# Layer 0's mixer: three pairs of column blocks with two seven-product units each

## The chip, the cores and the metric

The kernel runs on one core of a Trainium2 chip. The metric is the device time of one execution in microseconds (us), the median of several runs. The engines are named as in the profile: PE (TensorE's matmuls; PEld its weight loads), DVE (VectorE), ACT (ScalarE), POOL (GpSimd), SP (SyncE, which issues the weight loads).

## The reference, cut to what matters

A two-layer encoder over 256 tokens of width 2048, in fp32. Layer 0 mixes tokens by a chunked spatial gating and by attention to 256 memory tokens; layer 1 by grouped-query attention. Each layer ends with a SwiGLU FFN.

```python
h = rms_norm(x, g_mix[l])                       # (256, 2048)
z = h @ w_in_a                                  # layer 0: u 1536, v 1536, q_mem 512 columns
tok_in, q_mem = split(z, [3072])
u, v = split(gelu(tok_in), 2)
v = rms_norm(v, g_v_a)
s = einsum('gts,bcsgd->bctgd', w_spatial, v) + b_spatial
tok_out = u * s                                 # 1536 wide
mem_out = memory_attention(q_mem, mem, ...)     # 512 wide, 4 heads
x = x + concat([tok_out, mem_out]) @ w_out[l]   # 2048 x 2048
x = x + (silu(gate) * up) @ w_down[l]           # gate, up = split(rms_norm(x) @ w_gate_up[l])
```

## The kernel before, in words

**The matmul.** Activations and weights are fp32, split into two halves that TensorE takes at full speed: hi is a rounded copy, lo the rest. matmul3 (L185 to L189) makes three matmuls of a product: hi x hi, lo x hi, hi x lo. A weight tile `raw` (128 x 2048: four 128x512 pieces) is loaded by SP, its `whi` is a cast on ScalarE (L271), its `wlo` a subtraction on VectorE (L272). There are 3 buffers each of whi and wlo (W_TILES) and 4 of raw (RAW_TILES), so a half's making waits for PE to be done with the one three before it.

**Linear** (run at L288 and after) computes one block of 512 columns for both halves of the tokens (t = 0, 1) in two PSUM banks named `acc` out of four. It takes four units of four pieces of depth: 24 matmuls each, 96 a block. A tick of the program's clock passes after each 12; `later(n, f)` records work n ticks on.

**Pair** (L346 to L460) computes two neighbouring blocks, as the FFN does already. A unit is a 2 x 2 arrangement of weight pieces against a 2 x 2 arrangement of activations (two pieces of depth, two token halves). `eight` takes eight products, 24 matmuls; `seven`, for units in `fast`, takes seven, 21 matmuls, and needs sums: of weights in `prepare` (L380 to L382: T from raw, raw from T, T from raw, after which T's three pieces are halved as well as raw's four), and of activations (activation_sums, L318 to L333, from whole features that feature_sums, L825, adds up from their halves first). Products that both token halves share gather in two double banks from the pool `m`; after the last seven `inner` (L430 to L437) joins them into the tile `e`, and at the pair's end `outer` (L453 to L458) adds the four acc banks to e, which empties those banks for what comes next.

**Layer 0's mixer** runs thirteen Linears: v's three blocks, q_mem, the memory's keys and values, u's three blocks, w_out's four. v's blocks go through gelu and squares as they come (`gated`, L767 to L771); gate_rms and gate (L687 to L700) scale v and multiply it by the spatial matrices. Each of u's blocks goes through gelu on ScalarE (L787), is multiplied by the gate on VectorE (L788), and is turned (turn_u, L702): `turned` (L195) copies its 16-bit planes apart on VectorE (L200), turns them by a DMA transpose from ScalarE's queue (L201), and some ticks later copies them back (L206); `split` (L177 to L183) then makes hi (ScalarE, L181) and lo (VectorE, L182), which w_out's matmuls read. Because turning u's last block takes time, w_out's units start with the memory heads (pieces 12 to 15). The memory attention's steps are set at ticks (4, 16, 20, 28) after q_mem. add_residual (L645) adds a block of w_out to x and turns it for the FFN. The mixer's pool has 36 tiles (MIX_TILES), its `m` banks are four single ones.

**What sets the order.** The program is recorded as written, with the ticks; a scheduler then lists the instructions of each engine, by a simulated timeline of its own. On the chip each engine takes its list in that order, so an instruction that waits holds back all behind it. After layer 0's mixer comes the FFN (pairs throughout), then layer 1, not touched.

Of the kernel before, what the change touches and what calls it, by code (L numbers as in the profile page):

```python
# [10 lines left out]
F32 = mybir.dt.float32  # L11
# [6 lines left out]
P = 128  # L18
# [14 lines left out]
KC4 = 4  # L33
MIX_TILES = 36
FFN_TILES = 26
# [6 lines left out]
class Parts:  # L42


    def __init__(self):
        self.ap, self.whole = {}, {}

# [8 lines left out]
def encoder(ctx: ExitStack, tc: tile.TileContext, x, x_t, mem, mem_t, columns, w_in_a, g_v_a, spatial_t, w_in_b,  # L56
# [23 lines left out]

    def open_rooms(scope, name, tiles, banks):

        room["p"] = scope.enter_context(tc.tile_pool(name=name, bufs=tiles, reuse_waits="tile"))
        room["m"] = scope.enter_context(tc.tile_pool(name=f"ps_{name}", bufs=4 // banks, space=PS))
        room["banks"] = banks

    def banks2():
# [149 lines left out]
    def gained_pair(src, i, g, parts, keep):  # L237

        hi = keep(F32R, [P, 2, S])
        lo = keep(F32R, [P, 2, S])  # L240
        for c in range(2):
            gc = g[:, 2 * i + c:2 * i + c + 1]
            nc.scalar.activation(hi[:, c], src[:, c], AF.Copy, scale=gc)
            nc.vector.scalar_tensor_tensor(lo[:, c], src[:, c], gc, hi[:, c].bitcast(F32), ALU.mult, ALU.subtract)
            for t in range(NT):
                ts = slice(t * P, (t + 1) * P)
                parts.put(2 * i + c, t, hi[:, c, ts], lo[:, c, ts])

    class Norm:
# [68 lines left out]
    def activation_sums(a0, a1, apart=False):  # L318

        if apart:  # L320
            q = room["p"].tile([P, KC3, NB], F32, tag="T", name=nm("T"), bufs=2)[:, 0].rearrange("p (c n) -> p c n", n=P)
        else:
            q = big(F32, [P, 4, P])
# [17 lines left out]
    class Pair:  # L341
# [29 lines left out]
        def prepare(self, i):  # L371

            if i in self.ready:
                return
            raw = self.fetch(i)
            self.ready[i] = (raw,)
            if i in self.fast:
                T = room["p"].tile([P, KC3, NB], F32, tag="T", name=nm("T"), bufs=2)
                w01 = raw[:, 0].unsqueeze(1).to_broadcast([P, 2, NB])
                nc.vector.tensor_tensor(T[:, :2], raw[:, 1:4:2], w01, ALU.add)  # L380
                nc.vector.tensor_tensor(raw[:, 0], T[:, 0], raw[:, 3], ALU.add)
                nc.vector.tensor_tensor(T[:, 2], raw[:, 0], raw[:, 2], ALU.add)  # L382
                self.ready[i] = raw, T

# [278 lines left out]


    hT = Parts()
    norm = Norm()
    for l in range(DEPTH):
        scope = ExitStack()
        open_rooms(scope, f"mix{l}", MIX_TILES, 1)
        cat = Parts()  # L670
        m = Memory(l)
        if l == 0:
            w = w_in_a[0]
# [28 lines left out]
            def turn_u(us, t, c):  # L702
                def parts(whole):
                    hi, lo = split(whole, [P, 4, P])
                    for i in range(4):
# [61 lines left out]
            def gated(c, acc):  # L767
                for t in range(NT):
                    v[t][c] = big()
                    nc.scalar.activation(v[t][c], acc[t], AF.Gelu, scale=norm.r[t])  # L770
# [11 lines left out]
            m.values()  # L782
            for c in range(3):
                acc = linear(hT, w, c * NB)
# [27 lines left out]
        norm = Norm()  # L812
        units = kd if l else [(12, KC4), (0, KC4), (4, KC4), (8, KC4)]
        for j in range(4):
            acc = linear(cat, w_out[l], j * NB, units)
            add_residual(acc, j, norm, gslice("ffn", l), hF, j < 3, nc.scalar.copy if l else nc.vector.tensor_copy)
        room.clear()
        scope.close()
# [5 lines left out]

        def feature_sums(i):  # L825
            j, c = i // 2, 2 * (i % 2)
            whole = []
            for t in range(NT):
                hi, lo = hF.whole[j, t]
                a = big(F32, [P, 2, P])  # L830
                nc.vector.tensor_tensor(a, hi[:, c:c + 2].bitcast(F32), lo[:, c:c + 2].bitcast(F32), ALU.add)
                whole.append(a)
            sums[i] = activation_sums(*whole)

        for i in fast:
            later(2 + 2 * i, lambda i=i: feature_sums(i))

        hT = Parts()
        next_norm = Norm()
        for chunk in (range(0, 4), range(4, 8), range(8, 11)):  # L840
# [44 lines left out]
            for jj, g in enumerate(pairs):  # L885
                g.run(None if jj else pairs[1])
                for j in (2 * jj, 2 * jj + 1):
                    if last and l < DEPTH - 1:
                        residual_turns(j, next_norm, gslice("mix", l + 1), hT)
                    elif last:  # L890
                        for t in range(NT):
                            parts = 2 if j == 3 and t == NT - 1 else 1
                            for i in range(parts):
# [3 lines left out]
                                              X[t][j][:, cs])  # L897
        norm = next_norm
        room.clear()
        scope.close()  # L900
# [48 lines left out]
```

## Time and profile before

| what | value |
|---|---|
| median of 3 runs | 1989.67 us (1989.49 to 1989.98) |
| the profiled execution, its own time | 1992.44 us |
| its span, first to last instruction | 1990.7 us |
| granted TensorE clock | 1.0 |
| first matmul of v's second block | 28.61 us |
| of q_mem, the keys, the values | 73.60, 100.68, 122.53 us |
| of u's first, second block | 144.29, 170.59 us |
| of w_out's first, third block | 217.03, 260.55 us |
| of the FFN | 304.07 us |

In rows of the timeline the columns are start, duration, engine, line, operation, output<-inputs, and in brackets the idle time before it with what ended it. Groups give count, busy time, mean in ns, and the idle time before them. In windows come the length, the busy time (and count) of PE, PEld, DVE, ACT and POOL, the granted clock, the DMA share and GB/s. An instruction that follows another closely on DVE or ACT starts a little before that one's end as shown.

### The profile page before, as it was taken

Reading aid. Unit: us, or ns where it says so; the run is one execution under the profiler, and the core shown is the slowest. Engines: PE = TensorE matmul, PEld = TensorE weight load, DVE = VectorE, ACT = ScalarE, POOL = GpSimd, SP = SyncE. Lnnn points to the kernel's source line nnn. Section 1 sums busy time; section 2 is a strip of 40 time slices with the busy share of each in tenths; the row PEclk is TensorE's granted clock in tenths of the full one; section 3 lists DMA queues with packets and bytes.
Section 4 is the critical chain, followed back from the end, with each engine's and each line's share of the span. In section 5 each row is a group of like instructions: output and inputs, shape, how many; then the busy total and the mean of one; then the engine's idle time right before and its main releaser. Section 6 shows DMA issues by size and latency. Waiting matters only on the chain.

```text
span 1990.7 us, 24068 instructions
## 1 busy us (share of the span) xinstructions
PE 1978.8 (99%) x8913; PEld 1638.5 (82%) x8913; DVE 1648.7 (83%) x1783; ACT 1214.6 (61%) x1461; POOL 81.5 (4%) x122
## 2 busy tenths in 40 slices
PE   9999999999999999999999999999999999999998
PEld 7888888888887888888888888888888878888887
DVE  6668678998988989898676876699889889898887
ACT  8756555775546655466765755766664567644673
POOL 2300001000000000000011000010000000000000
PEclk9999999999999999999999999999999999999999
DMA  9867765676775767757866444747767667686674
GB/s 349 300 190 228 217 212 190 196 224 214 235 230 180 233 208 240 236 183 237 240 204 208 157 143 155 221 169 224 229 200 248 199 201 233 201 252 213 196 226 139
DMA packets 283495, 425.93 MB, mean 214 GB/s; under 512 B 89681, under 2 KB 89937, under 8 KB 283377
## 3 DMA queue, kind: packets, MB, share of 16 engines
q1 hardware_dynamic: 199808, 387.62, 58.6%
q10 hardware_dynamic: 78576, 19.86, 5.7%
q0 software_dynamic: 4992, 16.91, 3.8%
q8 instruction: 70, 1.15, 0.2%
q14 instruction: 49, 0.39, 0.1%
HBM read 394.45 MB, written 2.10 MB: 199 GB/s over the span
## 4 chain that ended last, share of the span: by engine, by line
PE 91%; DMA 3%; DVE 3%; issue 1%; ACT 1%; SPq 0%; DVEq 0%; ACTq 0%
PE acc L189 26%; PE acc L187 26%; PE acc L188 26%; PE m L189 4%; PE m L187 4%; PE m L188 4%; DMA a<-a 2%; DVE wlo L272 2%; DMA raw<-in_w_in_a 1%; ACT whi L271 1%; PE m L193 0%; PE m L561 0%; DMA raw<-in_w_down 0%; DMA raw<-in_w_gate_up 0%; PE m L698 0%
## 5 line engine op out<-in xcount | busy, mean ns | idle before, releaser
L272 DVE TENSOR_TENSOR wlo<-raw,whi 128x2048 fp32r<-128x2048 f32 (+2 forms) x466 | 841.7, 1823 | 214.0 <-ACT whi L271 206.9
L271 ACT CAST whi<-raw 128x2048 fp32r<-128x2048 f32 (+2 forms) x466 | 706.0, 1535 | 448.8 <-PE acc L188 317.8
L187 PE MATMUL acc<-whi,h 128*128 128x512 f32 x1440 | 561.0, 390 | 1.5 <-ACT whi L271 1.5
L188 PE MATMUL acc<-whi,h 128*128 128x512 f32 x1440 | 560.7, 389 | 0.0
L189 PE MATMUL acc<-wlo,h 128*128 128x512 f32 x1440 | 514.9, 390 | 1.3 <-DVE wlo L272 1.1
L187 PE MATMUL acc<-whi,a 128*128 128x512 f32 x999 | 388.6, 390 | 1.2 <-DVE x L458 1.2
L188 PE MATMUL acc<-whi,a 128*128 128x512 f32 x999 | 388.9, 390 | 0.0
L189 PE MATMUL acc<-wlo,a 128*128 128x512 f32 x999 | 365.5, 390 | 0.0
L189 PEld LDWEIGHTS acc<-wlo,h 128*128 128x128 f32 x1440 | 270.3, 188 | 58.8 <-DVE wlo L272 3.2
L187 PEld LDWEIGHTS acc<-whi,h 128*128 128x128 f32 x1440 | 270.4, 188 | 57.4 <-ACT whi L271 2.1
L188 PEld LDWEIGHTS acc<-whi,h 128*128 128x128 f32 x1440 | 270.4, 188 | 55.7
L187 PEld LDWEIGHTS acc<-whi,a 128*128 128x128 f32 x999 | 187.5, 188 | 40.5 <-issue 1.6
L189 PEld LDWEIGHTS acc<-wlo,a 128*128 128x128 f32 x999 | 187.6, 188 | 39.7 <-DVE wlo L272 0.9
L188 PEld LDWEIGHTS acc<-whi,a 128*128 128x128 f32 x999 | 187.6, 188 | 38.5
L271 ACT CAST whi<-T 128x1536 fp32r<-128x1536 f32 x93 | 137.8, 1482 | 120.4 <-PE acc L188 94.1
L272 DVE TENSOR_TENSOR wlo<-T,whi 128x1536 fp32r<-128x1536 f32 x93 | 163.3, 1756 | 4.7 <-PE acc L189 4.7
L380 DVE TENSOR_TENSOR T<-raw 128x1024 f32<-128x1024 f32 x93 | 113.7, 1222 | 17.2 <-DMA raw<-in_w_gate_up 17.1
L189 PE MATMUL m<-wlo,a 128*128 128x512 f32 x284 | 110.7, 390 | 0.3 <-DVE wlo L272 0.2
L187 PE MATMUL m<-whi,a 128*128 128x512 f32 x284 | 110.9, 391 | 0.1
L188 PE MATMUL m<-whi,a 128*128 128x512 f32 x284 | 110.5, 389 | 0.0
L458 DVE TENSOR_TENSOR e<-acc,e 128x512 f32<-128x512 f32 x120 | 79.5, 690 | 1.7 <-PE acc L189 1.3
L206 ACT COPY sg<-a 128x1024 uint16<-128x1024 uint16 x44 | 51.5, 1171 | 33.4 <-DMA a<-a 33.4
(145 smaller groups left out, 1520.1 us busy)
## 6 DMA issues: line engine op xcount, KB each, us to landing
raw<-in_w_gate_up SPq DMA_DIRECT2D x352, 512.0 KB, 4.4
raw<-in_w_down SPq DMA_DIRECT2D x176, 512.0 KB, 4.9
raw<-in_w_out SPq DMA_DIRECT2D x32, 1024.0 KB, 5.3
raw<-in_w_in_a SPq DMA_DIRECT2D x24, 1024.0 KB, 7.7
raw<-in_w_in_b SPq DMA_DIRECT2D x24, 1024.0 KB, 5.1
raw<-in_w_mem_kv SPq DMA_DIRECT2D x16, 1024.0 KB, 5.2
x<-e POOLq DMA_DIRECT2D x16, 512.0 KB, 5.1
a<-in_mem_t POOLq DMA_DIRECT2D x16, 256.0 KB, 4.3
```

Of the source, the lines that this page charges most:

```text
L187: nc.tensor.matmul(out, lhsT=a[0], rhs=b[0], start=start, stop=False)
L188: nc.tensor.matmul(out, lhsT=a[1], rhs=b[0], start=False, stop=False)
L189: nc.tensor.matmul(out, lhsT=a[0], rhs=b[1], start=False, stop=stop)
L206: copy(halves, back.rearrange("p (h n) -> p n h", h=2))
L271: nc.scalar.copy(hi[:, cut], raw[:, cut])
L272: nc.vector.tensor_tensor(lo[:, cut], raw[:, cut], hi[:, cut].bitcast(F32), ALU.subtract)
L380: nc.vector.tensor_tensor(T[:, :2], raw[:, 1:4:2], w01, ALU.add)
L458: nc.vector.tensor_tensor(o[t][n], self.bank[name], o[t][n], op)
```

## The change

v's second and third blocks, u's second and third, and w_out's first and second are each computed as one Pair of eight units, of which units 0 and 1 are sevens, at the fourth and sixth place (w_out: third and fourth, units 6 and 7, the memory heads, first). The sums for v and u are made from h in v's first block's wake and kept (`hsums`); those for w_out's sevens are made from u's first block (`csums`). Pairs need double banks, so the `m` pool is opened as two double banks, changed to four single ones for q_mem to u's first block, and back. v's first block is copied out of PSUM by VectorE as soon as it is done and gated later. Both of u's last blocks now come at the pair's end, and go through gelu, gate and turning together. w_out's first two blocks are added to x together. The memory attention's last step is set at tick 24 instead of 28, and u's second block is turned one tick earlier after its end. T's scratch has one buffer in the mixer. The number of PE's rows goes from 8744 to 8726, DVE's from 1550 to 1632, ACT's from 1092 to 1102; POOL has 126 and SP 389 in both. After layer 0's mixer the order is the same on all engines.

```diff
-MIX_TILES = 36
+MIX_TILES = (29, 36)
...
+    def block_sums(parts, i, apart=False):
+        whole = []
+        for t in range(NT):
+            if i in parts.pair:
+                both = [a[:, :, t * P:(t + 1) * P] for a in parts.pair[i]]
+            else:
+                both = [a[:, 2 * (i % 2):2 * (i % 2) + 2] for a in parts.whole[i // 2, t]]
+            a = big(F32, [P, 2, P])
+            nc.vector.tensor_tensor(a, both[0].bitcast(F32), both[1].bitcast(F32), ALU.add)
+            whole.append(a)
+        return activation_sums(*whole, apart)
...
+    def two(parts, sums, w, n0, order, fast):
+
+        g = Pair(parts, sums, w, n0, n0 + NB, order, fast)
+        g.run()
+        return [[g.out[t][n] for t in range(NT)] for n in range(2)]
...
-            later(7, lambda: gated(0, acc))
-            for c in (1, 2):
-                gated(c, linear(hT, w, TOK + c * NB))
+            whole = [big() for _ in range(NT)]
+            for t in range(NT):
+                nc.vector.tensor_copy(whole[t], acc[t])
+            later(7, lambda: gated(0, whole))
+            for i in range(2):
+                sums_later(hT, hsums, i, 4 + 2 * i, not i)
+            for c, acc_c in zip((1, 2), two(hT, hsums, w, TOK + NB, (2, 3, 4, 0, 5, 1, 6, 7), (0, 1))):
+                gated(c, acc_c)
+            open_banks("mix0", 1)
...
-            m.attend(linear(hT, w, 2 * TOK), norm.r, cat, (4, 16, 20, 28), True)
+            m.attend(linear(hT, w, 2 * TOK), norm.r, cat, (4, 16, 20, 24), True)
...
+                if c == 1:
+                    later(4, lambda: open_banks("mix0", 2))
+                    for i in range(2):
+                        sums_later(cat, csums, i, 10 + 2 * i)
+                    blocks = two(hT, hsums, w, NB, (2, 3, 4, 0, 5, 1, 6, 7), (0, 1))
+                acc = blocks[c - 1] if blocks else linear(hT, w, c * NB)
...
-                    later(1 + t, lambda u=u, t=t, c=c: turn_u(u, t, c))
+                    later(t + (c != 1), lambda u=u, t=t, c=c: turn_u(u, t, c))
...
+        if l == 0:
+            blocks = two(cat, csums, w_out[l], 0, (6, 7, 0, 1, 2, 3, 4, 5), (0, 1))
         for j in range(4):
-            acc = linear(cat, w_out[l], j * NB, units)
+            acc = blocks[j] if j < 2 and not l else linear(cat, w_out[l], j * NB, units)
```

Lines move by some ten: in the changed kernel whi and wlo are L283 and L284, the T sums L392 to L394, e's joining L446 to L449, its last additions L470, the two copies of turning L211 and L217 with the transpose at L212, split L192 and L193, the gelu of u L836 and its product L837, the residual L670.

**VectorE where w_out begins, before.** The names: wlo is the low half of a weight tile, `a` any 128x512 tile of the mixer (here u's last block); the first number is the tile's.

```order
L272 TENSOR_TENSOR wlo_336_1960<-raw_334_1957,whi_335_1959 128x1024 x2
L788 TENSOR_TENSOR a_321_1907<-a_321_1907,a_109_713 128x512
L200 COPY a_330_1937<-a_321_1907 128x1024
L272 TENSOR_TENSOR wlo_341_1997<-raw_339_1994,whi_340_1996 128x1024 x2
L788 TENSOR_TENSOR a_322_1910<-a_322_1910,a_110_717 128x512
L206 COPY a_321_1907<-a_331_1938 128x1024
L200 COPY a_332_1953<-a_322_1910 128x1024
L272 TENSOR_TENSOR wlo_346_2034<-raw_344_2031,whi_345_2033 128x1024 x2
L182 TENSOR_TENSOR a_338_1991<-a_321_1907,a_337_1990 128x512
L206 COPY a_322_1910<-a_333_1954 128x1024
L182 TENSOR_TENSOR a_343_2016<-a_322_1910,a_342_2015 128x512
```

**The same place after the change, rows 205 to 216** (T is the sum tile of w_out's first seven, wlo_389 its low half):

```order
L837 TENSOR_TENSOR a_354_1977<-a_354_1977,a_129_754 128x512
L837 TENSOR_TENSOR a_355_1980<-a_355_1980,a_130_758 128x512
L211 COPY a_364_2009<-a_352_1971 128x1024
L211 COPY a_366_2013<-a_353_1974 128x1024
L211 COPY a_368_2017<-a_354_1977 128x1024
L217 COPY a_352_1971<-a_365_2010 128x1024
L211 COPY a_372_2035<-a_355_1980 128x1024
L217 COPY a_353_1974<-a_367_2014 128x1024
L217 COPY a_354_1977<-a_369_2018 128x1024
L193 TENSOR_TENSOR a_379_2076<-a_352_1971,a_378_2075 128x512
L217 COPY a_355_1980<-a_373_2036 128x1024
L284 TENSOR_TENSOR wlo_389_2101<-T_375_2042,whi_388_2100 128x1536
```

Before, two tiles of u were turned here with weight halves between them; now four are turned in a row, and a weight half stands behind the last of their copies.

**VectorE at the end of u's pair, rows 184 to 193 after the change.** wlo_351 belongs to u's last unit, wlo_361 and wlo_377 to w_out's first two; e is the pair's joined tile; T_375 belongs to w_out's first seven; acc_297 is the first bank that w_out's first unit takes over.

```order
L284 TENSOR_TENSOR wlo_351_1940<-raw_347_1908,whi_350_1939 128x2048
L447 TENSOR_TENSOR e_346_1903<-m_325_1787,e_346_1903 128x512
L336 TENSOR_TENSOR a_343_1894<-a_342_1892 128x128
L337 TENSOR_TENSOR a_343_1894<-a_342_1892,a_341_1890 128x128
L284 TENSOR_TENSOR wlo_361_1992<-raw_358_1985,whi_360_1991 128x2048
L392 TENSOR_TENSOR T_375_2042<-raw_374_2039 128x1024
L448 TENSOR_TENSOR e_346_1903<-m_326_1800,e_346_1903 128x1024
L338 TENSOR_TENSOR a_343_1894<-a_341_1890,a_343_1894 128x128
L284 TENSOR_TENSOR wlo_377_2047<-raw_359_1988,whi_376_2046 128x2048
L470 TENSOR_TENSOR e_346_1903<-acc_297_1643,e_346_1903 128x512
```

None of this but the weight halves was here before: a Linear's banks were read by ScalarE's gelu. Now the bank is emptied by the last row, behind the others.

**ScalarE where w_out begins, before:**

```order
L787 ACTIVATE a_321_1907<-acc_299_1759,s1_59_447 128x512
L271 CAST whi_340_1996<-raw_339_1994 128x1024 x2
L787 ACTIVATE a_322_1910<-acc_300_1760,s1_62_453 128x512
L201 DMA_TRANSPOSE a_331_1938<-a_330_1937 128x8x128
L271 CAST whi_345_2033<-raw_344_2031 128x1024 x2
L201 DMA_TRANSPOSE a_333_1954<-a_332_1953 128x8x128
L181 CAST a_337_1990<-a_321_1907 128x512
```

**And after, rows 147 to 158** (whi_388 and whi_395 are the high halves of w_out's first seven's T and its second seven's raw):

```order
L836 ACTIVATE a_354_1977<-e_346_1903,s1_71_470 128x512
L836 ACTIVATE a_355_1980<-e_346_1903,s1_74_476 128x512
L212 DMA_TRANSPOSE a_365_2010<-a_364_2009 128x8x128
L212 DMA_TRANSPOSE a_367_2014<-a_366_2013 128x8x128
L212 DMA_TRANSPOSE a_369_2018<-a_368_2017 128x8x128
L212 DMA_TRANSPOSE a_373_2036<-a_372_2035 128x8x128
L192 CAST a_378_2075<-a_352_1971 128x512
L283 CAST whi_388_2100<-T_375_2042 128x1536
L192 CAST a_380_2080<-a_353_1974 128x512
L192 CAST a_382_2085<-a_354_1977 128x512
L192 CAST a_391_2118<-a_355_1980 128x512
L283 CAST whi_395_2135<-raw_384_2089 128x2048
```

The gelus read e instead of a bank; the four transposes and a cast stand ahead of whi_388, and four casts of u ahead of whi_395.

More of the change, by code (lines that the diff above doesn't have):

```diff
@@ L45, in __init__ @@
     def __init__(self):
-        self.ap, self.whole = {}, {}
+        self.ap, self.whole, self.pair = {}, {}, {}
     def put(self, kc, t, hi, lo):
@@ L79, in small, with open_rooms, open_banks, close_banks @@
         return sp.tile([P, n], F32, tag=f"{'r' if long else 's'}{n}", name=nm(f"s{n}"), bufs=8 if long else 6)
-    def open_rooms(scope, name, tiles, banks):
+    def open_rooms(scope, name, tiles, banks, scratch=2):
         room["p"] = scope.enter_context(tc.tile_pool(name=name, bufs=tiles, reuse_waits="tile"))
-        room["m"] = scope.enter_context(tc.tile_pool(name=f"ps_{name}", bufs=4 // banks, space=PS))
+        room["scratch"] = scratch
+        open_banks(name, banks)
+    def open_banks(name, banks):
+        close_banks()
+        room["psum"] = ExitStack()
+        room["m"] = room["psum"].enter_context(tc.tile_pool(name=nm(f"ps_{name}"), bufs=4 // banks, space=PS))
         room["banks"] = banks
+    def close_banks():
+        if "psum" in room:
+            room.pop("psum").close()
     def banks2():
@@ L247, in gained_pair @@
                 parts.put(2 * i + c, t, hi[:, c, ts], lo[:, c, ts])
+        parts.pair[i] = hi, lo
     class Norm:
@@ L662, in residual_turns, with sums_later, make @@
         add_residual(None, j, norm, g, parts, j < 2)
+    def block_sums(parts, i, apart=False):
[9 more added lines that the diff above has]
+        return activation_sums(*whole, apart)
+    def sums_later(parts, sums, i, wait, apart=False):
+        def make():
+            sums[i] = block_sums(parts, i, apart)
+        later(wait, make)
+    def two(parts, sums, w, n0, order, fast):
+        g = Pair(parts, sums, w, n0, n0 + NB, order, fast)
+        g.run()
+        return [[g.out[t][n] for t in range(NT)] for n in range(2)]
     hT = Parts()
@@ L668, in encoder @@
         scope = ExitStack()
-        open_rooms(scope, f"mix{l}", MIX_TILES, 1)
+        open_rooms(scope, f"mix{l}", MIX_TILES[l], 1 if l else 2, 1)
         cat = Parts()
         m = Memory(l)
+        hsums, csums = {}, {}
         if l == 0:
@@ L704, in parts @@
                     hi, lo = split(whole, [P, 4, P])
+                    cat.whole[c, t] = hi, lo
                     for i in range(4):
@@ L768, in gated @@
                 for t in range(NT):
-                    v[t][c] = big()
+                    v[t][c] = acc[t] if not c else big()
                     nc.scalar.activation(v[t][c], acc[t], AF.Gelu, scale=norm.r[t])
                     square_sum(v[t][c], ssv[t][:, 2 * c:2 * c + 2])
-            later(7, lambda: gated(0, acc))
-            for c in (1, 2):
-                gated(c, linear(hT, w, TOK + c * NB))
+            whole = [big() for _ in range(NT)]
[7 more added lines that the diff above has]
+            open_banks("mix0", 1)
             for t in range(NT):
@@ L779, in encoder @@
                     later(3 + 3 * t + c, lambda t=t, c=c: gate(t, c))
-            m.attend(linear(hT, w, 2 * TOK), norm.r, cat, (4, 16, 20, 28), True)
+            m.attend(linear(hT, w, 2 * TOK), norm.r, cat, (4, 16, 20, 24), True)
             m.keys()
             m.values()
+            blocks = []
             for c in range(3):
-                acc = linear(hT, w, c * NB)
+                if c == 1:
[4 more added lines that the diff above has]
+                acc = blocks[c - 1] if blocks else linear(hT, w, c * NB)
                 for t in range(NT):
@@ L823, in encoder @@
         fast = (0, 1, 2)
[L825 to L833, printed above, removed]
         for i in fast:
-            later(2 + 2 * i, lambda i=i: feature_sums(i))
+            sums_later(hF, sums, i, 2 + 2 * i)
         hT = Parts()
@@ L898, in encoder @@
         norm = next_norm
+        close_banks()
         room.clear()
```

5 lines of the change are left out of this document (3 added, 2 removed).

## The prediction

> **What bounds the kernel now.** I read the page first, then the windows of the stages that the change rewrites, then single rows. On the page, the engines' busy time:
>
> ```profile
> PE 1978.8 (99%) x8913; PEld 1638.5 (82%) x8913; DVE 1648.7 (83%) x1783; ACT 1214.6 (61%) x1461; POOL 81.5 (4%) x122
> ```
>
> TensorE is the bound; every microsecond it stands idle, and every matmul it is spared, shows in the time. The windows, by stage: v's last two blocks, u's last two, w_out's first two, and a stretch of the FFN, which is made of pairs already:
>
> ```profile
> 28.00:74.00 46.00, 45.13 (x198) 36.75 (x197) 24.00 (x26) 35.77 (x79) 17.85 (x39) 1.00 1.03 364
> 170.00:217.00 47.00, 47.00 (x220) 39.39 (x219) 35.32 (x42) 24.66 (x30) 0.00 (x0) 1.00 0.73 218
> 217.00:261.00 44.00, 44.00 (x195) 36.41 (x194) 31.34 (x41) 22.69 (x38) 0.00 (x0) 1.00 0.71 219
> 700.00:800.00 100.00, 100.00 (x442) 82.47 (x441) 88.11 (x75) 55.21 (x39) 1.72 (x2) 1.00 0.74 227
> ```
>
> After the length come PE, PEld, DVE, ACT and POOL, busy. PE is full but for 0.87 us in the first row; DVE is half to three quarters full in the three stages and 88 of 100 in the FFN, where PE still loses nothing. So pairs at 88% DVE can be free. The last row gives the pace: 100/442 = 0.226 us, and 0.2267 between starts over longer stretches, for one 128x512 matmul. The clock column is 1.00.
>
> **What is removed.** A seven does 21 matmuls where an eight does 24. Two sevens in each of three pairs: 6 x 3 = 18 matmuls, 18 x 0.2267 = **-4.1 us**. As 0.2% is about what a measurement of this kernel can tell from no change (4.0 us of 1989.67), even the whole gain would hardly be seen.
>
> **What is added: VectorE work.** The FFN's first pairs have all its kinds:
>
> ```profile
> L272 DVE TENSOR_TENSOR wlo<-raw,whi 128x2048 fp32r<-128x2048 f32 x22 | 50.4, 2291 | 5.6 <-ACT whi L271 5.6
> L272 DVE TENSOR_TENSOR wlo<-T,whi 128x1536 fp32r<-128x1536 f32 x8 | 14.0, 1756 | 0.0
> L380 DVE TENSOR_TENSOR T<-raw 128x1024 f32<-128x1024 f32 x9 | 11.0, 1221 | 0.6 <-DMA raw<-in_w_gate_up 0.6
> L381 DVE TENSOR_TENSOR raw<-T,raw 128x512 f32<-128x512 f32 x9 | 6.2, 688 | 0.0
> L382 DVE TENSOR_TENSOR T<-raw 128x512 f32<-128x512 f32 x8 | 5.5, 689 | 0.0
> L458 DVE TENSOR_TENSOR e<-acc,e 128x512 f32<-128x512 f32 x8 | 5.3, 691 | 0.0
> ...
> L436 DVE TENSOR_TENSOR e<-m,e 128x1024 f32<-128x1024 f32 x2 | 2.4, 1220 | 0.0
> L831 DVE TENSOR_TENSOR a<-h,h 128x256 f32<-128x256 f32 x6 | 2.3, 419 | 0.0
> L435 DVE TENSOR_TENSOR e<-m,e 128x512 f32<-128x512 f32 x3 | 2.1, 685 | 0.0
> ...
> L326 DVE TENSOR_TENSOR a<-a,a 128x128 f32<-128x128 f32 x5 | 1.4, 286 | 0.0
> ```
>
> And instructions that follow each other closely start sooner than these durations say:
>
> ```profile
> 163.31 1.22 DVE L272 TENSOR_TENSOR wlo<-raw,whi 128x1024 fp32r<-128x1024 f32 x1
> 164.45 0.69 DVE L200 COPY a<-a 128x1024 uint16<-128x1024 uint16 x1
> 165.05 1.22 DVE L272 TENSOR_TENSOR wlo<-raw,whi 128x1024 fp32r<-128x1024 f32 x1
> ```
>
> 1.22 takes a place of 1.14 in the queue, 0.69 one of 0.60. I use these places: 2.2 for wlo of 2048, 1.67 for wlo of T, 1.14, 0.60, about 0.34 for L831 and 0.2 for L326's kind. Two column blocks cost DVE 16 x 1.22 = 19.6 us of weight halves before; as a pair 8 x 2.29 + 2 x 1.76 for halves, 2 x (1.22 + 0.69 + 0.69) for T, 5.4 for joining the parts in e (0.69 + 1.22 + 0.69 + 4 x 0.69), and 2 x 2.7 for sums of activations (2 x 0.42 + 4 x 0.29 + 0.69): 37.8. That is 18 us more in each stage of 186 x 0.2267 = 42.2 us. With 24.0, 35.3 and 31.3 busy before, v's stage stands at 42, u's at 53 and w_out's at 49: DVE becomes as long as PE there or longer. Work must slide into neighbours, and the order of its queue decides which matmul waits.
>
> **v's pair: +2.4.** Before, PE loses time here already, since the second unit's cast waits behind squares on ScalarE (PE's timeline, starts; one step is 0.2267):
>
> ```profile
> 33.83 0.39 PE L189 MATMUL acc<-wlo,h 128*128 128x512 f32 x1
> 34.99 0.50 PE L187 MATMUL acc<-whi,h 128*128 128x512 f32 x1 [0.77 <-ACT whi L271]
> 35.33 0.40 PE L188 MATMUL acc<-whi,h 128*128 128x512 f32 x1
> 35.56 0.39 PE L187 MATMUL acc<-whi,h 128*128 128x512 f32 x1
> 35.79 0.40 PE L188 MATMUL acc<-whi,h 128*128 128x512 f32 x1
> 36.28 0.50 PE L189 MATMUL acc<-wlo,h 128*128 128x512 f32 x1
> 36.62 0.40 PE L187 MATMUL acc<-whi,h 128*128 128x512 f32 x1
> ```
>
> Six steps in 2.79 us: 2.79 - 1.36 = 1.4 lost. ScalarE right after:
>
> ```profile
> 35.80 0.41 ACT L213 ACTIVATE junk<-x 128x256 f32<-128x256 f32 x1
> 36.11 0.19 ACT L213 ACTIVATION_READ_ACCUMULATOR junk<-x 128x1 f32 x1
> 36.32 1.28 ACT L770 ACT_TABLE_LOAD   x1
> 37.61 0.69 ACT L770 ACTIVATE a<-acc,s 128x512 f32<-128x512 f32 x1
> 38.20 1.99 ACT L271 CAST whi<-raw 128x1024 fp32r<-128x1024 f32 x2
> ```
>
> Afterwards the second unit's cast is one piece of 1.9 us, still behind 14 squares: it ends at about 35.3 where PE arrives at 34.05, a loss of 1.35, plus 0.1 restart. Then the wlo of that unit (0.5), the third unit, whose cast stands behind the table load and a gelu (0.4), the second seven's T sums (0.5), and 0.95 at q's start, whose first bank is emptied by an e row that stands behind two weight halves of q. Sum 3.8, less the 1.4 that go: +2.4. Bounds: 0 (same loss as now) to +4.
>
> **u's pair: +1.8.** The first seven's weight half is DVE's first row behind the two copies (L217) that bring u's first block back from its transposes; these arrive 0.7 late. The second seven's T sums stand behind that half, the one from T, a split and the half of the unit after, 2.2 + 1.67 + 0.6 + 2.2 us that could be done earlier only if the copies were: its raw half is cast 1.05 late. Bounds: 0, if both transposes land at the quick end, to +3.
>
> **w_out's start: +2.75.** The front part's DVE rows 184 to 193 stand here in the queue. Let P be the end of u's last matmul. The second seven's whi ends as PE takes it up, 68 matmuls before P, at -15.4. From there DVE works without a pause: three halves to -9.3, the sums of w_out's first block to -8.0, wlo_351 -5.8, an e row and two sums -4.8, wlo_361 -2.6, T_375 -1.5, e row 190 -0.3, a sum -0.1, wlo_377 +2.1, and row 193, which empties the bank, +2.7. PE's first w_out matmul wants that bank at P. Here the end of the range is 0 (no DVE lag) below and about 4 above.
>
> **w_out's first seven: +6.0; its second: +4.35.** What u's end needs is now in one heap in front of them. ScalarE's and DMA's rows:
>
> ```profile
> L271 ACT CAST whi<-raw x466: 611/1907/1927, 5.5 to 1973.6; 128x2048 fp32r<-128x2048 f32 x88, 128x1024 fp32r<-128x1024 f32 x66, 128x512 fp32r<-128x512 f32 x2
> L271 ACT CAST whi<-T x93: 1467/1483/1491, 315.9 to 1968.9; 128x1536 fp32r<-128x1536 f32 x93
> ```
>
> ```profile
> L201 ACTq DMA_TRANSPOSE a<-a x11: 1247/1248/1302, 162.1 to 239.1; - x11
> ...
> DMA to landing us min/median/max: 3.1/3.7/5.8
> ```
>
> Walk on from row 193 at P + 2.7, by queue places: T and e rows to 6.5, wlo_387 8.7, a split 9.3, four products u*sb 11.7, three copies (L211) 13.5; row 210 waits for the first transpose (issued at 12.35, landed 15.9) 16.6; the fourth copy 17.2. Only now does the fourth transpose leave ScalarE's queue (1.25 us, 18.4), then a cast 19.0, then **whi_388**, row 154: 20.5. Wlo_389, DVE row 216, stands behind row 215, which waits for that fourth transpose (17.2 + 3.7 and more, 21 to 22): it ends at **23.4**. PE, late by 2.75, comes to whi_388 after 60 matmuls, at 16.35, and to wlo_389 four later: gaps of 4.15 and 1.9. The second seven's T sums (rows 219, 221, 222) come behind wlo_389 and two splits, the last that its raw half needs at 26.9; its cast ends at 28.8, PE is there at 24.5: 4.3. Behind it the halves come just in time (wlo_396 at 31.0, wanted at 31.07).
>
> The two gaps' bounds: 0, and 1.5 more each. Everything else I put at nothing: POOL's program does not grow, the weights come in the same bytes on SP's queue, and after layer 0's mixer every engine's order is as before. Two added copies of v's first block (0.7 each on DVE) lie where DVE has room, under v's pair. The memory heads' moved steps lie under u's first block, 96 matmuls or 22 us of it; -1 to +1, should that cover fail or serve better.
>
> **Sum.** -4.1 + 2.4 + 1.8 + 2.75 + 6.0 + 4.35 = +13.2. The profiled execution took 1992.44, its span 1990.7, and lies 2.8 above the median of the runs, 1989.67; the terms are the span's, and I add them to the median: **2003 us**.
>
> **Rivals.** *The cover holds*: the window 700:800 has DVE at 88% without loss; if copies and transposes come through quickly enough that wlo_389 ends within 13.6 us of P (60 matmuls), and DVE is not late at P, only the removed work counts, with v's old 1.4 at most gained too: 1984.2 to 1985.6. Against it stands a queue of 23 us, of which two landings are a quarter. Chance 0.10; this is the other side. *Half of it*: DVE lags as said, but the last two gaps (10.4) vanish, since the transposes do not hold the queue: 1992.6, about as likely just inside 0.2% as outside. Chance 0.22. *Slow transposes*: in the chain of waits one took
>
> ```profile
> 135.87 9.38 DMA a<-a
> ```
>
> and the fourth at 9 instead of 4 moves wlo_389 and all behind it by 5 to 8 more: 2008 to 2011, chance 0.10. *Cold restarts*: the first 24 small matmuls, after idle, against 24 later ones:
>
> ```profile
> 1.35 4.62 PE L724 MATMUL m<-ident 128*128 128x128 f32 x24 [1.35 <-POOL ident masks.py:199]
> ```
>
> ```profile
> 89.02 2.84 PE L698 MATMUL m<-a,a 128*128 128x128 f32 x24
> ```
>
> 1.8 us lost at a start from idle. If each gap of over 4 us ends in such a start, two of them add 3.6: 2006.5, chance 0.13. [...]
>
> **How the numbers follow.** The forecast has 0.45, its own range 1997 to 2009. Below it the half case is wholly inside the range and the covered one outside; above, only the worst of the slow transposes lies outside: 1988 to 2013. Faster by over 0.2% (below 1985.7): the covered case, 0.10. Within 0.2%: half of the half case and a little, 0.12. Slower by over 0.2% (above 1993.7): 0.78.
>
> **What would show it.** In the profile afterwards: PE idle of about 17 us between 28 and 261, none added later; the largest gaps some 14 and 20 us into w_out, the first ended by ScalarE's whi from T and DVE's wlo from T, the second by whi from raw; a gap of 2 to 3 us at w_out's first matmul, ended by DVE's e row; DVE at 90% or more from 170 to 261; the granted clock 1.00 in every stage, lower behind the long gaps if the cold rival is right. The prediction is wrong if PE is full in the last window, or if w_out's first seven starts on time.

## The result, and the profile after

| kernel | median, us | runs | ratio to before |
|---|---|---|---|
| before | 1989.83 | 1989.49 to 1990.11 (4) | |
| changed | 2007.52 | 2005.83 to 2008.54 (4) | 1.0084, 95% interval 1.0072 to 1.0095 |

The change makes the kernel slower by 17.7 us, well beyond 0.2%; forecast were 13.2. (The two medians alone give a ratio of 1.0089; 1.0084 is the estimate that the interval belongs to.) The profiled executions took 1992.44 and 2008.28 us, spans 1990.7 and 2006.5: 15.8 apart, and it is these 15.8 that the traces can account for. TensorE's share on the page is as before:

```profile
PE 1982.7 (99%) x8895; PEld 1637.0 (82%) x8895; DVE 1693.2 (84%) x1834; ACT 1225.4 (61%) x1450; POOL 88.7 (4%) x122
```

18 matmuls fewer, 45 us more of VectorE, and yet PE is busy 4 us longer, which is a first hint of slow matmuls. The windows of v's pair, u's pair, w_out's pair and w_out's last two blocks, in the changed kernel:

```profile
28.00:74.00 46.00, 44.68 (x191) 34.81 (x189) 39.50 (x48) 38.95 (x76) 26.34 (x39) 1.00 1.02 360
170.00:217.00 47.00, 43.84 (x200) 34.88 (x199) 39.03 (x44) 24.58 (x22) 0.00 (x0) 1.00 0.59 167
217.00:270.00 53.00, 43.97 (x172) 34.42 (x171) 43.15 (x45) 21.76 (x20) 0.00 (x0) 0.87 0.62 185
270.00:320.00 50.00, 50.00 (x222) 41.39 (x221) 41.49 (x64) 31.56 (x67) 0.00 (x0) 1.00 0.74 222
```

The second and third rows hold the loss: 3.2 and 9.0 us without a matmul, and in the third a granted clock of 0.87. The last row is full. VectorE is busy 83% and 81% of the bad rows, not all of them: it waits too. By the starts of the stages' first matmuls, the time between the two traces goes like this:

| stage | before | after | difference |
|---|---|---|---|
| to v's second block | 28.61 | 28.94 | +0.33 |
| v's pair | 44.99 | 45.35 | +0.36 |
| q_mem to u's first block | 96.99 | 95.43 | -1.56 |
| u's pair, to its last matmul | 46.44 | 49.77 | +3.33 |
| w_out's first matmul late | 0 | 2.39 | +2.39 |
| w_out's first two blocks | 43.52 | 54.15 | +10.63 |
| w_out's last two blocks | 43.52 | 43.52 | 0 |
| the rest | 1686.63 | 1686.95 | +0.32 |

What TensorE waited for, in all (the columns are total, times, longest):

```profile
PE m L198 <- ACT whi L283: 8.4, 5, 3.6
PE acc L198 <- DVE e L470: 2.8, 2, 2.2
PE acc L198 <- DVE x L470: 1.8, 1, 1.8
PE acc L200 <- DVE wlo L284: 1.7, 5, 0.6
PE m L200 <- DVE wlo L284: 1.5, 2, 1.3
```

PE's timeline at w_out's first matmul, at its first seven's whi from T and at its second seven's whi:

```profile
219.26 0.39 PE L200 MATMUL acc<-wlo,h 128*128 128x512 f32 x1
221.88 0.47 PE L198 MATMUL acc<-whi,a 128*128 128x512 f32 x1 [2.23 <-DVE e L470]
...
235.37 0.39 PE L200 MATMUL acc<-wlo,a 128*128 128x512 f32 x1
239.38 0.79 PE L198 MATMUL m<-whi,a 128*128 128x512 f32 x1 [3.62 <-ACT whi L283]
239.97 0.63 PE L199 MATMUL m<-whi,a 128*128 128x512 f32 x1
240.40 0.63 PE L198 MATMUL acc<-whi,a 128*128 128x512 f32 x1
...
243.47 0.63 PE L200 MATMUL acc<-wlo,a 128*128 128x512 f32 x1
247.13 0.79 PE L198 MATMUL m<-whi,a 128*128 128x512 f32 x1 [3.03 <-ACT whi L283]
247.72 0.63 PE L199 MATMUL m<-whi,a 128*128 128x512 f32 x1
```

After the two long gaps the matmuls start 0.427 us apart (239.97 to 240.40) instead of 0.227, until 251.56. VectorE's timeline in front of the first of them, from the copies of u's turning to wlo_389:

```profile
230.65 1.89 DVE L211 COPY a<-a 128x1024 uint16<-128x1024 uint16 x3
234.72 0.69 DVE L217 COPY a<-a 128x1024 uint16<-128x1024 uint16 x1 [2.17 <-DMA a<-a]
235.33 0.69 DVE L211 COPY a<-a 128x1024 uint16<-128x1024 uint16 x1
236.15 0.69 DVE L217 COPY a<-a 128x1024 uint16<-128x1024 uint16 x1
237.43 0.69 DVE L217 COPY a<-a 128x1024 uint16<-128x1024 uint16 x1 [0.58 <-DMA a<-a]
238.04 0.68 DVE L193 TENSOR_TENSOR a<-a,a 128x512 fp32r<-128x512 f32 x1
239.19 0.69 DVE L217 COPY a<-a 128x1024 uint16<-128x1024 uint16 x1 [0.46 <-DMA a<-a]
239.80 1.75 DVE L284 TENSOR_TENSOR wlo<-T,whi 128x1536 fp32r<-128x1536 f32 x1
```

And ScalarE's, with whi_388 behind the four transposes and a cast:

```profile
231.37 5.92 ACTq L212 DMA_TRANSPOSE a<-a  x4
237.33 0.62 ACT L192 CAST a<-a 128x512 fp32r<-128x512 f32 x1 [9.96 <-DMA a<-a]
237.86 1.47 ACT L283 CAST whi<-T 128x1536 fp32r<-128x1536 f32 x1
```

With u's last matmul ended at 219.49 (P), whi_388 is there at P + 19.8 (forecast 20.5) and wlo_389 at P + 22.1 (23.4).

### The profile page after: what moved, and what is told of

Its sections match the earlier page's. It is cut to its first block, busy times and chain, and to the rows that moved or that the text cites. A ratio compares the mean times of both kernels' runs of the same rounds, so it can differ in the third digit from the quotient of the medians.

```text
span 2006.5 us, 24153 instructions
## 1 busy us (share of the span) xinstructions
PE 1982.7 (99%) x8895; PEld 1637.0 (82%) x8895; DVE 1693.2 (84%) x1834; ACT 1225.4 (61%) x1450; POOL 88.7 (4%) x122
## 4 chain that ended last, share of the span: by engine, by line
PE 84%; DVE 5%; DMA 4%; issue 3%; ACT 2%; ACTq 0%; SPq 0%; DVEq 0%
PE acc L200 24%; PE acc L198 23%; PE acc L199 23%; PE m L198 4%; PE m L199 4%; PE m L200 4%; DMA a<-a 3%; DVE wlo L284 2%; ACT whi L283 2%; DMA raw<-in_w_in_a 1%; DMA raw<-in_w_down 1%; DVE T L392 1%; DVE e L470 0%; PE m L204 0%; DMA a<-in_x_t 0%
## 5 line engine op out<-in xcount | busy, mean ns | idle before, releaser
L284 DVE TENSOR_TENSOR wlo<-raw,whi 128x2048 fp32r<-128x2048 f32 (+2 forms) x442 | 839.6, 1911 | 191.9 <-ACT whi L283 185.9
L283 ACT CAST whi<-raw 128x2048 fp32r<-128x2048 f32 (+2 forms) x442 | 703.9, 1609 | 458.3 <-PE acc L199 311.8
L198 PE MATMUL acc<-whi,h 128*128 128x512 f32 x1416 | 551.7, 390 | 1.3 <-ACT whi L283 0.6
L199 PE MATMUL acc<-whi,h 128*128 128x512 f32 x1416 | 551.4, 389 | 0.0
L200 PE MATMUL acc<-wlo,h 128*128 128x512 f32 x1416 | 502.2, 390 | 1.5 <-DVE wlo L284 1.3
L198 PEld LDWEIGHTS acc<-whi,h 128*128 128x128 f32 x1416 | 265.9, 188 | 56.5 <-ACT whi L283 1.4
L199 PEld LDWEIGHTS acc<-whi,h 128*128 128x128 f32 x1416 | 265.9, 188 | 54.8
L283 ACT CAST whi<-T 128x1536 fp32r<-128x1536 f32 x99 | 146.7, 1482 | 119.8 <-PE acc L199 98.1
L284 DVE TENSOR_TENSOR wlo<-T,whi 128x1536 fp32r<-128x1536 f32 x99 | 173.4, 1751 | 4.7 <-PE acc L200 4.7
L392 DVE TENSOR_TENSOR T<-raw 128x1024 f32<-128x1024 f32 x99 | 120.7, 1219 | 17.9 <-DMA raw<-in_w_gate_up 15.9
L198 PE MATMUL m<-whi,a 128*128 128x512 f32 x298 | 117.6, 395 | 6.7 <-ACT whi L283 6.6
L200 PE MATMUL m<-wlo,a 128*128 128x512 f32 x298 | 116.9, 392 | 0.3 <-DVE wlo L284 0.2
L199 PE MATMUL m<-whi,a 128*128 128x512 f32 x298 | 116.9, 392 | 0.0
L470 DVE TENSOR_TENSOR e<-acc,e 128x512 f32<-128x512 f32 x132 | 87.1, 684 | 1.6 <-PE acc L200 1.3
L198 PEld LDWEIGHTS m<-whi,a 128*128 128x128 f32 x298 | 56.6, 190 | 20.6 <-ACT whi L283 9.2
```

The costliest lines, as they stand in the source:

```text
L198: nc.tensor.matmul(out, lhsT=a[0], rhs=b[0], start=start, stop=False)
L199: nc.tensor.matmul(out, lhsT=a[1], rhs=b[0], start=False, stop=False)
L200: nc.tensor.matmul(out, lhsT=a[0], rhs=b[1], start=False, stop=stop)
L283: nc.scalar.copy(hi[:, cut], raw[:, cut])
L284: nc.vector.tensor_tensor(lo[:, cut], raw[:, cut], hi[:, cut].bitcast(F32), ALU.subtract)
L470: nc.vector.tensor_tensor(o[t][n], self.bank[name], o[t][n], op)
```

## The experiments

Three questions were open. First, whether the loss belongs to the place where u's and w_out's pairs meet (the junction theory, the forecast's), or to each pair by itself, since it gives VectorE more work than its stage holds (the load theory). Second, whether the slow matmuls are the gaps' doing. Third, and later, whether it is work or waits on VectorE's queue that cost (work against hold).

Two readings stand for each run: the median against before's runs on the same chip, which there lay between 1987.5 and 1997.7 us for one kernel (but for one of 8465.53 us, which is left out); and the delay in layer 0, the time from the first unit's first matmul to that of the FFN's seventeenth weight tile, in one traced execution, less before's 382.07 us. The second is the sharper one within layer 0: in the nine traces whose program is the same up to u's pair, that pair's first matmul lies 162.7 to 163.4 us after the first unit's. After the delay's end the executions lost between 6 and 15 us of matmul time in scattered gaps of the FFN and layer 1. This was 12 to 15 us in the five traces with late sevens or without u's pair but with w_out's, and 6 to 11 us in the others; whether these runs push loss out of layer 0 or had bad luck isn't settled, and the delay doesn't count it.

| run | median - before's, us | ratio, 95% interval | delay in layer 0, us | clock |
|---|---|---|---|---|
| the change | +17.7 | 1.0072 to 1.0095 | +15.4 | 0.997 |
| w_out's pair undone | +7.5 | 1.0028 to 1.0058 | +5.8 | 0.999 |
| u's pair undone | +7.5 | 1.0031 to 1.0069 | +5.1 | 1.0 |
| v's pair alone | +0.3 | 0.9991 to 1.0012 | +0.7 | 1.0 |
| w_out's pair one block later | +23.1 | 1.0099 to 1.0131 | +19.1 | 0.996 |
| u's turning copies on ScalarE | +8.6 | 1.0024 to 1.0048 | +6.9 | 0.998 |
| late sevens, without the pair's last additions | +8.7 | 1.0026 to 1.0059 | +8.1 | 1.0 |
| TensorE kept busy in the gaps | +12.7 | 1.0043 to 1.0076 | +12.8 | 0.999 |
| late sevens, u's pair undone, without the last additions | +8.3 | 1.0029 to 1.0057 | +3.8 | 0.998 |
| only the copy apart on ScalarE | +8.5 | 1.0025 to 1.0064 | +10.4 | 0.998 |
| only the copy back on ScalarE | +10.1 | 1.0036 to 1.0068 | +13.2 | 0.945 |
| late sevens, whole | +8.7 | 1.0030 to 1.0065 | +4.3 | 0.999 |
| u's pair undone, copies on ScalarE | +11.5 | 1.0034 to 1.0080 | +7.3 | 0.997 |

**w_out's pair undone.**

```diff
-                    for i in range(2):
-                        sums_later(cat, csums, i, 10 + 2 * i)
...
-            blocks = two(cat, csums, w_out[l], 0, (6, 7, 0, 1, 2, 3, 4, 5), (0, 1))
+            pass
...
-            acc = blocks[j] if j < 2 and not l else linear(cat, w_out[l], j * NB, units)
+            acc = linear(cat, w_out[l], j * NB, units)
```

> v's and u's pairs stay, w_out's first two blocks are Linears again. Junction theory (four turnings, T sums and bank emptying of two pairs back to back hold the queues where w_out begins, and the gaps of over 3.5 us there slow the clock): the 10.6 us of w_out's first two blocks go, a gap of 2 to 3 us at w_out's first matmul may stay, clock 1.000; 1992 to 1996 us. Load theory (each pair overloads VectorE and costs about a third of the 17.7 us, wherever it stands): about 2001.5 us.

Measured: 1997.85 us, between the two. The gap at w_out's first matmul is gone (0.13 us), so this part of the junction came from w_out's own T, sums and halves in VectorE's queue. What is left there is a wait for u itself, and slow matmuls behind it:

```profile
231.92 0.79 PE L198 MATMUL acc<-whi,a 128*128 128x512 f32 x1 [2.47 <-ACT a L192]
232.65 0.79 PE L199 MATMUL acc<-whi,a 128*128 128x512 f32 x1
```

The third unit wants u's second block, which in a pair comes out together with the third and is turned with it: two units of matmuls no longer cover the turning.

**u's pair undone.**

```diff
-                if c == 1:
+                if c == 2:
                     later(4, lambda: open_banks("mix0", 2))
...
-                        sums_later(cat, csums, i, 10 + 2 * i)
-                    blocks = two(hT, hsums, w, NB, (2, 3, 4, 0, 5, 1, 6, 7), (0, 1))
-                acc = blocks[c - 1] if blocks else linear(hT, w, c * NB)
+                        sums_later(cat, csums, i, 1 + 2 * i)
+                acc = linear(hT, w, c * NB)
...
-                    later(t + (c != 1), lambda u=u, t=t, c=c: turn_u(u, t, c))
+                    later(1 + t, lambda u=u, t=t, c=c: turn_u(u, t, c))
```

> v's and w_out's pairs stay, u's blocks are Linears. Junction theory: only two tiles of u are turned where w_out begins, its first bank is free as before, the gaps at w_out's first seven shrink below 1.5 us, clock 1.000; 1988 to 1993 us. Load theory: about 2001.5 us.

Measured: 1997.84 us, again between. The first seven starts nearly on time (0.6 us late); the second waits for its whi as long as in the change, on PE's timeline:

```profile
234.65 0.39 PE L200 MATMUL acc<-wlo,a 128*128 128x512 f32 x1
238.56 0.50 PE L198 MATMUL m<-whi,a 128*128 128x512 f32 x1 [3.53 <-ACT whi L283]
238.90 0.39 PE L199 MATMUL m<-whi,a 128*128 128x512 f32 x1
```

The sum that this cast needs ends at 236.5, behind the copies back of u's last block and between its splits on VectorE's queue. And after 3.5 us of idle time the matmuls are not slow (0.34 to the next start, then 0.23).

**v's pair alone.** As the two above together.

> Only v's pair, and the memory heads' last step at tick 24. Junction theory: v's pair costs about what it saves (stage 45.35 us after against 44.99 before), the two gaps of 1.4 us that before had at the memory heads may go or stay; 1988 to 1991 us. Load theory: a third of the loss, about 1995.7 us.

Measured: 1990.67 against 1990.37 us: no difference. v's pair pays back what it saves, as the junction theory said. By the delays in layer 0, u's pair costs 5.8 - 0.7 = 5.1 on top of it, w_out's 5.1 - 0.7 = 4.3, and both together 15.4 - 0.7 = 14.7: 5.3 us belong to their meeting. By the medians the same sum gives 7.2 for each and 3.0 for the meeting, and the four intervals, each 2 to 4 us wide to either side, don't tell 3.0 from nothing. What holds by both readings: neither a third for each pair (v's costs nothing) nor the junction alone (each of the other two costs without it) is right. That the meeting adds anything rests on the delays.

**w_out's pair one block later.**

```diff
-            blocks = two(cat, csums, w_out[l], 0, (6, 7, 0, 1, 2, 3, 4, 5), (0, 1))
+            first = linear(cat, w_out[l], 0, units)
+            add_residual(first, 0, norm, gslice("ffn", l), hF, True, nc.vector.tensor_copy)
+            blocks = two(cat, csums, w_out[l], NB, (6, 7, 0, 1, 2, 3, 4, 5), (0, 1))
-        for j in range(4):
-            acc = blocks[j] if j < 2 and not l else linear(cat, w_out[l], j * NB, units)
+        for j in range(1 - l, 4):
+            acc = blocks[j - 1] if 0 < j < 3 and not l else linear(cat, w_out[l], j * NB, units)
```

> All three pairs, but w_out's first block is a Linear and its second and third are the pair, so 96 matmuls or 21.8 us of TensorE lie between u's pair and the pair of w_out. Junction theory: the turnings go under the Linear and the gaps at the sevens vanish, a gap of 2 to 3 us at w_out's first matmul stays, clock 1.000; 1991 to 1996 us. Load theory: as the change, 2005 to 2009 us.

Measured: 2013.49 us, worse than the change. The junction theory's remedy fails: the scheduler drew the pair's first half and T sums forward into the Linear, where the copies of u's turning still stood, and PE waited within it (its timeline):

```profile
231.26 0.39 PE L200 MATMUL acc<-wlo,a 128*128 128x512 f32 x1
234.80 0.79 PE L198 MATMUL acc<-whi,a 128*128 128x512 f32 x1 [3.15 <-ACT whi L283]
```

Later the turning of w_out's first block into the FFN's input met the sevens' T sums instead of u's. So the matmuls put between did not shorten the queue, which the scheduler filled anew.

**u's turning copies on ScalarE.**

```diff
-                turned(us, 3, parts, True, nc.vector.tensor_copy)
+                turned(us, 3, parts, True)
```

> The change, with the two copies of every turning of u on ScalarE instead of VectorE (12 copies). Load theory (VectorE has more work than TensorE has in u's and w_out's pairs): 12 x 0.6 us leave VectorE, 8 of them between u's end and w_out's sevens, and 4 to 6 us of the loss go: 2001.5 to 2003.5 us. Queue theory (what counts is that work stands behind waits for transposes): the same waits now hold ScalarE's queue with the casts in it, so no gain or worse: 2007 us or more.

Measured: 1999.83 us, against before 9.1 us less than the change and by the delay in layer 0 8.5 less, more than the load theory had said. The windows of w_out's first part, in the change and in this run:

```profile
217.00:276.00 59.00, 49.97 (x198) 39.40 (x197) 47.51 (x51) 23.76 (x22) 0.00 (x0) 0.88 0.61 184
```

```profile
217.00:276.00 59.00, 54.34 (x224) 43.61 (x223) 47.86 (x51) 38.57 (x46) 0.00 (x0) 0.94 0.69 201
```

Both VectorE's work and its waits for transposes had been moved at once; two more runs were made to part them.

**Only the copy apart, only the copy back on ScalarE.**

```diff
-    def turned(src, ticks, then, over=False, copy=nc.scalar.copy):
+    def turned(src, ticks, then, over=False, copy=nc.scalar.copy, back_copy=None):
...
-            copy(halves, back.rearrange("p (h n) -> p n h", h=2))
+            (back_copy or copy)(halves, back.rearrange("p (h n) -> p n h", h=2))
...
-                turned(us, 3, parts, True, nc.vector.tensor_copy)
+                turned(us, 3, parts, True, nc.scalar.copy, nc.vector.tensor_copy)
```

> The change, with only the first copy of each turning of u (planes apart) on ScalarE; the copy back, which waits for the transpose, stays on VectorE. Work theory (it is VectorE's amount of work that costs): 6 x 0.6 us of VectorE's work go from u's and w_out's stages, half of what the run with both copies moved took away, and about half of its gain comes: 2003 to 2005 us. Hold theory (it is VectorE's queue standing still behind the copy back that costs): the waits stay, 2005 to 2008 us.

> The change, with only the copy back of each turning of u on ScalarE, so that VectorE waits for no transpose of u. Work theory: as with the first copy moved, 2003 to 2005 us. Hold theory: all of the gain that both copies gave, 1999 to 2001 us.

(The second run has the two copies the other way round.) Measured: 2000.3 and 2001.91 us. The first gains more than half and has its waits still (VectorE stands 3.6 us before the first copy back), so the hold theory in its plain form falls. By the delay in layer 0 it gains 5.0 of the 8.5 us that both copies gave, near the half that the work theory said; by the median it gains all of it (9.2 against 9.1), and misses the work theory's time too. The medians of these three runs, 8.5 to 10.1 above before, can't be told apart. The second shows that a hold is not removed when it moves to ScalarE. Its timelines of PE and ScalarE in u's pair:

```profile
191.16 0.39 PE L200 MATMUL acc<-wlo,h 128*128 128x512 f32 x1
194.50 0.79 PE L198 MATMUL m<-whi,h 128*128 128x512 f32 x1 [2.95 <-ACT whi L283]
```

```profile
191.49 1.16 ACT L217 COPY a<-a 128x1024 uint16<-128x1024 uint16 x1 [6.32 <-DMA a<-a]
192.55 1.89 ACT L283 CAST whi<-raw 128x2048 fp32r<-128x2048 f32 x1
194.35 1.47 ACT L283 CAST whi<-T 128x1536 fp32r<-128x1536 f32 x1
```

A copy back waits 6.3 us for its transpose, and the casts that TensorE wants stand behind it. So by the delays neither half gives all, and the split between work and hold is not settled: work seems to count everywhere, a hold where something urgent stands behind it. The scheduler also orders each of these programs anew, and no run changes one of the two alone.

**u's pair undone, copies on ScalarE.** The run without u's pair, with both copies of u's turning on ScalarE.

> v's and w_out's pairs, u as Linears, with both copies of u's turning on ScalarE. If the 3.7 us gap before w_out's sevens comes from VectorE's turnings (work or wait): it falls below 1.5 us and the time to 1992 to 1995 us. If w_out's pair costs by its own sums: 1997 to 1999 us, as without u's pair before.

Measured: 2003.37 us, against before 4.0 us more than without the move (the intervals overlap) and by the delay 2.2 more; both forecasts missed. The copies take 1.05 and 1.17 us each on ScalarE against 0.69 on VectorE, and here they bring ScalarE's casts behind waits:

```profile
229.85 1.17 ACT L217 COPY a<-a 128x1024 uint16<-128x1024 uint16 x1 [3.06 <-DMA a<-a]
229.86 1.25 ACTq L212 DMA_TRANSPOSE a<-a  x1
231.15 0.62 ACT L192 CAST a<-a 128x512 fp32r<-128x512 f32 x1
231.67 1.47 ACT L283 CAST whi<-T 128x1536 fp32r<-128x1536 f32 x1
```

PE waits 2.0 us for this last cast, and the matmuls behind it are slow (0.43 us from the first start to the next); it waits 2.2 us again for the second seven's.

**Late sevens.** First in two forms whose last unit was a seven, so that the four banks of the pair's end were never added into e: these two kernels leave that part of w_out's first two blocks out (four VectorE additions). Then whole, with an eight last, which is the edit shown; the first two forms have the order (6, 7, 0, 1, 2, 4, 3, 5), and the second has u's blocks as Linears too.

```diff
-                    for i in range(2):
-                        sums_later(cat, csums, i, 10 + 2 * i)
...
-            blocks = two(cat, csums, w_out[l], 0, (6, 7, 0, 1, 2, 3, 4, 5), (0, 1))
+            for i in (4, 5):
+                sums_later(cat, csums, i, 2 * i - 2)
+            blocks = two(cat, csums, w_out[l], 0, (6, 7, 0, 1, 2, 4, 5, 3), (4, 5))
```

> The change, with units 4 and 5 (u's last block) as w_out's sevens, at the sixth and eighth place, so that no T sum or half of T is made while u is turned. Queue theory: the gaps before w_out's third and fourth unit (4.0 and 3.7 us with their slow matmuls, 11.6 in all) go, and at most 3 us come back where the last block's sums are late: 1996 to 2000 us, clock 1.000. Load theory: VectorE's work is the same and so is the loss in the pair, only later: 2005 us or more.

> v's and w_out's pairs, u's blocks as Linears, w_out's sevens units 4 and 5 at the sixth and eighth place. Queue theory: the gap of 3.7 us that the run without u's pair had before w_out's sevens goes: 1993 to 1995 us. Load theory: as without u's pair, 1997 to 1999 us.

> The change, with units 4 and 5 as w_out's sevens at the sixth and seventh place and an eight last, so that the whole of the pair is computed. If the loss belongs to T sums standing behind turnings: no gap over 1.5 us in w_out's first two blocks, 1998 to 2001 us. If it belongs to VectorE's amount of work: what is spared there comes back as gaps in w_out's last blocks and the FFN's first pairs, 2001 to 2005 us.

Measured: 1999.94, 1999.47 and 2000.56 us. With u's pair, moving the sevens away from the turnings wins 9.0 us against before and 11.1 by the delay in layer 0 (15.4 to 4.3, whole form). No T and no sums of w_out stand in u's pair any more, and w_out's first matmul is on time. The window:

```profile
217.00:276.00 59.00, 55.79 (x239) 44.02 (x238) 54.03 (x68) 30.69 (x36) 0.00 (x0) 1.00 0.67 200
```

VectorE is 92% busy there and TensorE still loses 3.2 us, 2.0 of them in one gap: the whole form came in the time forecast for it, but with a gap over the 1.5 us that its forecast allowed. So the order at the junction was worth about half of the loss or more. That what remains is VectorE's load is a reading of its 92% and was not tried by itself. Without u's pair the same move wins nothing that can be measured (1999.47 after 1997.84): no gap is left in the pair, but 0.4, 1.4 and 1.0 us come back in the FFN's first pair.

**TensorE kept busy.** Eight matmuls of a zero piece, which add nothing, stand in the gaps; each is two records in the trace.

```diff
+            fill = getattr(self, "idle", {}).get(i, (0, 0))
...
+                for _ in range(fill[n]):
+                    nc.tensor.matmul(self.bank[2][:64], lhsT=ident[:64, 64:],
+                                     rhs=self.spare[:64],
+                                     start=False, stop=False)
...
-            blocks = two(cat, csums, w_out[l], 0, (6, 7, 0, 1, 2, 3, 4, 5), (0, 1))
+            blocks = two(cat, csums, w_out[l], 0, (6, 7, 0, 1, 2, 3, 4, 5), (0, 1), {0: (0, 4), 1: (4, 0)})
```

> The change, with eight more matmuls that add nothing (a zero 64x64 piece of the identity), four standing before the first matmul that wants whi_388 and four before the wlo of that tile, so that TensorE works in most of the two long gaps. If the gaps cause the slow matmuls after them: clock 1.000 and 3.5 to 4 us less, 2003.5 to 2004.5 us. If the slow clock has another cause, or is only a reading: 2007 to 2010 us, clock 0.997.

Measured: 2003.88 us with more matmuls than the change has, against before 5.0 us less than the change (the two intervals just overlap), and 2.6 less by the delay in layer 0. PE's timeline there:

```profile
236.38 0.39 PE L200 MATMUL acc<-wlo,a 128*128 128x512 f32 x1
236.70 3.64 PE L430 MATMUL acc<-a,ident 64*64 64x512 f32 x8
240.28 0.50 PE L198 MATMUL m<-whi,a 128*128 128x512 f32 x1
240.62 0.40 PE L199 MATMUL m<-whi,a 128*128 128x512 f32 x1
```

Behind the filled gaps the matmuls run at full pace (0.23 to 0.24 us apart after the first), so the idle time was what slowed them; that is shown. The clock is 0.999 and not 1.000 (0.95 from 217 to 250 us), since nine matmuls were slow, wholly or in part, behind the idle time of 2.26 us at w_out's first matmul, which the change's own trace did not show.

## Why the prediction was right, step by step

- **The sign and most of the size.** Forecast +13.2, measured +17.7 (15.8 between the profiled executions). The main case happened, and with it the rival of the cold restarts, which had been given 0.13 on its own and priced at +3.6. That the sum came so near is in part luck: u's pair (+2.9 over its term) and the slow matmuls (+4.4) were too low or left out, and the sevens (-2.8), v's pair (-0.7), w_out's start (-0.4) and the memory heads' stretch (-1.6) came out lower than forecast. PE's idle time between v's second block and w_out's third was 13.8 us, not 17.
- **The removed work**, -4.1: 8913 records less 8895 are the 18 matmuls.
- **v's pair**, +2.4: its stage grew by 0.36 with 1.36 removed, so +1.7. Right in place, a little too high.
- **u's pair**, +1.8, was mis-sized: its stage grew by 3.33 with 1.36 removed, +4.7. One copy back of u's first block waited 4.5 us for its transpose (VectorE's row below), and the half behind it stopped TensorE for 1.3 us instead of 0.7. And the copies back of the memory heads' transposes, one of them 7.05 us on its way in the chain of waits, stand in front of the halves of the pair's second and third unit: gaps of 0.8 and 0.5, where before had none. This second part belongs to the step that put the memory heads at nothing, -1 to +1. On the other side before's two gaps at their scores, 1.4 in all, are gone, and the stretch from q_mem to u's first block came out at -1.56, outside that bound.

```profile
190.81 1.35 DVE L217 COPY a<-a 128x1024 uint16<-128x1024 uint16 x2 [4.51 <-DMA a<-a]
```

- **w_out's start**, +2.75: measured 2.39, ended by the e row that was named.
- **w_out's two sevens**, +10.35: the gaps were 3.8, 0.4 and 3.4, so 7.6 in all; whi_388 and wlo_389 came 0.7 and 1.3 us earlier than the walk along the queue said, and TensorE came to wlo_389 some 0.4 us later, since the matmuls before it were slow. So the second gap was 0.4 and not 1.9. The order of events was the forecast one.
- **The slow matmuls** were weighed as a rival and not put in the sum. They are 10.63 + 1.36 - 7.6 = 4.4 us with the restarts. The run with TensorE kept busy has 2.6 us less delay by its trace, with 1.6 (nine matmuls, seven of them 0.2 late) lost anew at w_out's first matmul.
- **The other rivals.** The cover did not hold; the last gaps did not vanish; the four transposes were not the slow kind: from issue to landing they took 3.2 us in the median, and they left ScalarE's queue in 5.92 us. DVE at 90% was wrong: it was 83% and 81% busy, since it waited as well.
- **What the forecast's reason missed** is that the junction is only a part of it. By the delays u's and w_out's pairs cost 4 to 5 us each without the other, and only 5.3 on top, a third, belong to their meeting; by the medians each costs 7 and the meeting's part is within the noise. Not tried was to issue u's transposes from another queue than ScalarE's, where they stand in front of whi_388.

No version tried beat the kernel before; the nearest, v's pair alone, equals it.

## What to carry to other kernels

Fewer matmuls are worth their time only where the engine that pays for them has room in that stage and in that order: here 4.1 us of TensorE were bought with 45 us more of VectorE's busy time, in a queue that also waits for transposes. A walk along the in-order queues, row by row with the trace's durations, gave w_out's gaps to within 0.4 to 1.6 us each, where the queue was known; ask of every moved step what it waits for in its new place. Where two heavy stages meet, keeping the sums away from the turnings took 11 of the 15 us of delay away, more than any move of the copies to another engine. By the medians it gained 9.0 us, as much as moving both of u's copies to ScalarE (9.1).

## What the runs showed of the hardware

The pace fell to about half (0.427 us from start to start instead of 0.227) after some gaps and not after others, and length alone doesn't tell which. It fell after 3.62 us of idle time in the change, where it was still at half behind the next gap, of 3.03 us; it fell after 2.47 us in the run without w_out's pair, and not after 3.53 us in the run without u's pair. After 2.23 us at w_out's first matmul it did not fall in the change, and fell in the run with u's copies on ScalarE, 0.9 us after the start, for some 3 us; with TensorE kept busy and with only the copy apart on ScalarE it fell there too, after 2.26 and 2.24 us. PE's timeline of the run with u's copies on ScalarE:

```profile
219.60 0.47 PE L198 MATMUL acc<-whi,a 128*128 128x512 f32 x1 [2.23 <-DVE e L470]
...
220.49 0.63 PE L198 MATMUL acc<-whi,a 128*128 128x512 f32 x1
220.92 0.63 PE L199 MATMUL acc<-whi,a 128*128 128x512 f32 x1
```

The falls after 2.23 and 2.47 us, and the 3.53 us without one, don't fit a bound on one gap's length. What the fall does depend on was not tried.

The granted clock can also read low without a loss: in the traced execution with only the copy back on ScalarE it was 0.95 from 320 to 1990 us, while TensorE took as many matmuls there (7504 records in 1670 us) as the run with only the copy apart did at 1.00 (7501).
